# A hybrid attention and conv layer on one core: value sums emptied by VectorE, one more key block per pair through the DMA transpose, and the output projection begun inside the attention's last steps

## The chip, the core and the metric

One core of a Trainium2 chip runs the whole program. The metric is the device time of one execution in microseconds (us); for the kernel before it is the median of three runs. One further execution was recorded by the profiler, and all durations below come from it. TensorE is PE in the rows (PEld its weight loads), VectorE is DVE, ScalarE is ACT, GpSimd is POOL, and SP is the queue that issues nearly all transfers.

## What is computed

The layer has 2048 tokens of 1024 channels. Eight attention heads of 64 channels and 512 channels of a short gated convolution are computed from one projection of the normed input, joined, multiplied by `w_out` and added to the input through a gate; a feed-forward part follows.

```python
mod = (c_act @ w_ada + b_ada)[:, None, :]
sh1, sc1, g1, sh2, sc2, g2 = jnp.split(mod, N_MOD, axis=-1)
...
attn = forgetting_attention(q, k, v, logf).reshape(b, s, ATTN_WIDTH)
conv = bg * causal_dwconv(cg * xin, conv_mix_w)
mixed = jnp.concatenate([attn, conv], axis=-1)
x = x + g1 * (mixed @ w_out)
h2 = rmsnorm(x, norm2_g) * (1 + sc2) + sh2
u = causal_dwconv(h2 @ w_up, ffn_conv_w)
u_gate, u_val = jnp.split(u, 2, axis=-1)
y = (jax.nn.silu(u_gate) * u_val) @ w_down
return x + g2 * y
```

The attention is causal; a query block of 128 rows sees the key blocks up to its own, and a running sum of log-sigmoids is added to the logits before the softmax.

## The kernel before

Nearly every product is made in three passes: an operand is split into a high and a low part, and the products high by high, high by low and low by high are summed (`mm3`, L138). A split is one ScalarE copy into `hi` and one VectorE subtraction into `lo` (`split`, L865). An order that is wrapped in `K(...)` stays as the code writes it on its engine; other instructions are placed by a scheduler.

**Attention (L645 to L830).** The work is cut into 64 units, eight for each head. A unit is two query blocks, number 15-u and number u, which together see 17 key blocks. A unit goes through four stages in four successive steps of the loop at L798, so in step s four units are in work:

- `scores` of unit s (L690): PE makes the logits in chunks of up to 512 keys into four PSUM buffers (`product`, two chunks at a time), and VectorE adds the forget term and takes the maximum into `s_t` (L706), five chunks to a unit.
- `weights` of unit s-1 (L716): ScalarE forms the bias `nb` (L720) and takes the exponential of `s_t` in place, once for each of the two query blocks (L723).
- `turn` of unit s-2 (L727): the 17 blocks are transposed. The first WB = 10 go through PE (`blocks`, L743) in groups of 4, 4 and 2 into one of two PSUM buffers `pt`; ScalarE copies them to fp16 (L745), and VectorE subtracts to get the low part (`rest`, L750), which frees `pt`. The other 7 are split by GpSimd into `wide` (L734, L735) and turned by one DMA transpose from `wide` into `far` (L736, issued by SP). A reciprocal of the sums follows (L762).
- `values` of unit s-4 (L764): three products for each key block are summed into `po` (two PSUM buffers, one for each query block in turn); ScalarE empties each by one scaled copy into `at` (L781).

Inside a step the loop L823 goes round the stages, in the order turn, scores, weights, values, and lets each go on to its next `yield`; a step has five to seven rounds. Every second head, `store` (L784) turns a finished 512 columns of a pair of heads through `pt` and `tm` and writes it to `m_at` in DRAM, one piece to a step at four steps. At u = 1 to 7 of a head SP loads the next head's keys and queries, and GpSimd copies two of them (L594).

After step 63 come eight steps (s = 64 to 71) that only drain the stages.

**Output projection (`mixed`, L881).** Quarter Q takes 512 tokens. For each half `hf` of the 1024 outputs and each of eight input pieces k, in the order 4, 5, 6, 7 (from the convolution, `m_cv`) and 0, 1, 2, 3 (from the attention, `m_at`), it splits the weight piece `wo` and the input piece `src` and makes 12 products of 128x512 into four sums `acc`; pieces 2 and 3 are done together. In quarter 0 each `wo` is loaded (L908) and multiplied by the gate on GpSimd (L909) first. `mixed(0)` is called when the attention's program is at its end (L1176), followed by quarters 1 to 3 with the second norm between, and then the feed-forward part (`up`, `down`).

Of the kernel before, what the change touches and what calls it, by code (L numbers as in the profile page):

```python
# [19 lines left out]
P = 128  # L20
# [14 lines left out]
WB = 10  # L35
# [9 lines left out]
def kernel(  # L45
# [60 lines left out]
    qk = const.tile([P, 6], F32, name="qk")  # L106
# [537 lines left out]

    with ExitStack() as ph:  # L645
# [118 lines left out]
        def values(un):  # L764

            near, far = un["t"]
            h = un["h"]
            for p, (i, n, b0) in enumerate(un["parts"]):
# [11 lines left out]
                o = un["at"][:, i, (h % 2) * DH : (h % 2 + 1) * DH]  # L780
                K(A.activation(o, po, AF.Copy, scale=un["l"][:, p : p + 1]))  # L781
                yield

        def store(at, pr, chs):  # L784

            for ch in chs:
# [3 lines left out]
                tm = cp.tile([P, 512], F32, tag="tm", name="tm", bufs=2)  # L790
# [7 lines left out]
        for s in range(H * nu + 8):  # L798
# [29 lines left out]
        for g in slow:  # L828
# [10 lines left out]
    with ExitStack() as ph:  # L839
        fp = ph.enter_context(tc.tile_pool(name="fp", bufs=1))  # L840
        fp.tile([P, 32], F32, name="rim")
        fb = ph.enter_context(tc.tile_pool(name="fb", bufs=1))
# [3 lines left out]
        def raw_tile():  # L846
            return fq.tile([P, 1024], F32, tag="raw", name="raw", bufs=4)

        def pair_tiles():
            return (  # L850
                fq.tile([P, 1024], F32R, tag="hi", name="hi", bufs=4),
                fq.tile([P, 1024], F32R, tag="lo", name="lo", bufs=4),
            )

        def halves(tiles):

            return [[t[:, n * 512 : (n + 1) * 512] for t in tiles] for n in range(2)]
# [6 lines left out]

        def split(raw, hi, lo):  # L865
            A.activation(hi, raw, AF.Copy, scale=HS)  # L866
            V.tensor_tensor(lo, raw, hi.bitcast(F32), op=ALU.subtract)  # L867
            return hi, lo
# [9 lines left out]

        wo, kept = {}, {}

        def mixed(Q, side=iter(()), at=()):  # L881

            cols = slice(Q * 512, (Q + 1) * 512)
            order = (4, 5, 6, 7, 0, 1, 2, 3)
            rows = [slice((Q * 4 + t) * P, (Q * 4 + t + 1) * P) for t in range(4)]
            n = 0
            src = {}
            if Q < 2:
                spare = [(f"t{1 + i // 4}", i % 4, e) for e in "hl" for i in range(12)]
                for i, k in enumerate(order):  # L890
                    name, j, e = spare[8 * Q + i]
                    src[k] = (fb if name == "t3" else fp).tile([P, 512], F32, tag=f"{name}{j}{e}", name="src")
            else:
                for i in range(4):
                    raw = raw_tile()
                    for j in range(2):
                        src[order[2 * i + j]] = raw[:, j * 512 : (j + 1) * 512]
            if Q == 0:
                kept[0] = [raw_tile() for _ in range(4)]
                kept[1] = [wide_temp()[:, 0:D] for _ in range(4)]  # L900
            for hf in range(2):
                n0 = hf * 512
                acc = [ps_d.tile([P, 512], F32, tag="d", name="acc") for _ in range(4)]
                ops = []
                for k in order:
# [310 lines left out]
```

## Time and profile before

| what | value |
|---|---|
| median of three runs | 2559.99 us (2558.88 to 2562.83) |
| the profiled execution, its own time | 2562.44 us |
| its span, first to last instruction | 2560.5 us |
| granted TensorE clock, mean | 0.992 |
| attention, first to last `nb` (L720) | 630.8 to 963.1 us |
| first product of `mixed(0)` | 983.09 us |

The span lies within the execution's own time; 1.9 us lie around it. A row of the table of stages gives, for each engine, busy time and in brackets the number of instructions, then the granted clock, the share of the 16 DMA engines and GB/s. A row of a group gives line, engine, operation, what is written and read, the shape, the count, then busy time and the mean ns of one, and after the second bar the engine's idle time just before such instructions, with what ended it. A row of the timeline gives start, duration, engine, line, and in square brackets idle time and what ended it.

### The profile page before, as it was taken

What the parts mean: (1) busy time and instruction counts of PE and PEld (TensorE: products, weight loads), DVE (VectorE), ACT (ScalarE), POOL (GpSimd) and SP (SyncE); (2) the same over time, 40 slices, a digit from 0 to 9 for tenths busy, and PEclk for the clock granted to TensorE, in tenths of its full rate; (3) what the DMA queues carried; (4) which work ended last, traced back from release to release, by engine and by line L of the source; (5) the groups of instructions that cost most, each with busy time, mean ns of one, the idle gap of its engine ahead of it and who ended that gap; (6) DMA issues with size and microseconds to landing.
All of it is one profiled execution on the core that took longest, in us unless ns stands there. A gap on an engine that the chain in (4) does not pass through costs nothing.

```text
span 2560.5 us, 38478 instructions
## 1 busy us (share of the span) xinstructions
PE 2458.1 (96%) x14493; PEld 1995.7 (78%) x14493; DVE 1820.9 (71%) x3294; ACT 1183.2 (46%) x1932; POOL 357.8 (14%) x314
## 2 busy tenths in 40 slices
PE   4999999999999998998999999999999999999999
PEld 4988788887677776877888888877778888888887
DVE  7567874433888886676888888667768888885554
ACT  3522231111899994654444444455434444444333
POOL 4211010112656554110000000000000000000000
PEclk9999999999999999999999999999999999999999
DMA  8332563314697757332222222676632222226775
GB/s 237 140 104 59 153 177 103 99 54 122 122 187 154 162 96 236 116 111 94 83 83 74 83 83 83 210 233 209 218 125 75 86 80 81 81 84 191 226 234 188
DMA packets 400291, 341.43 MB, mean 133 GB/s; under 512 B 166545, under 2 KB 310249, under 8 KB 399081
## 3 DMA queue, kind: packets, MB, share of 16 engines
q1 hardware_dynamic: 392920, 322.13, 44.2%
q10 hardware_dynamic: 4752, 8.46, 0.9%
q0 software_dynamic: 2432, 8.39, 0.9%
q8 instruction: 113, 1.85, 0.3%
q14 instruction: 74, 0.60, 0.1%
HBM read 244.47 MB, written 65.08 MB: 121 GB/s over the span
## 4 chain that ended last, share of the span: by engine, by line
PE 50%; DVE 2%; DMA 1%; ACT 1%; issue 0%; SPq 0%; DVEq 0%; ACTq 0%
PE acc L1068 34%; PE acc L140 16%; DMA t<-x_sc 1%; DVE lo L867 1%; PE pt L956 0%; DVE t L949 0%; DVE t L876 0%; DVE t L875 0%; ACT junk L979 0%; ACT hi L866 0%; DVE b22l L867 0%; DVE lo L1023 0%; DVE t L966 0%; ACT t L958 0%; DVE w L986 0%
## 5 line engine op out<-in xcount | busy, mean ns | idle before, releaser
L140 PE MATMUL acc<-hi 128*128 128x512 f32 x960 | 378.2, 394 | 13.5 <-ACT hi L866 11.7
L140 PE MATMUL acc<-hi,lo 128*128 128x512 f32 x960 | 376.6, 392 | 0.8 <-DVE lo L867 0.7
L140 PE MATMUL acc<-lo,hi 128*128 128x512 f32 x960 | 375.9, 392 | 0.3 <-DVE lo L867 0.3
L867 DVE TENSOR_TENSOR lo<-raw,hi 128x1024 fp32r<-128x1024 f32 (+1 forms) x208 | 236.2, 1142 | 182.3 <-ACT hi L866 181.8
L866 ACT ACTIVATE hi<-raw 128x1024 fp32r<-128x1024 f32 (+1 forms) x208 | 205.0, 991 | 247.6 <-PE acc L140 207.6
L1081 DVE SCALAR_TENSOR_TENSOR w<-w,fcw,w 128x1024 f32<-128x1024 f32 x176 | 225.9, 1284 | 42.4 <-ACT w L1076 39.1
L1020 ACT ACTIVATE hi<-raw 128x1024 fp32r<-128x1024 f32 x132 | 139.4, 1057 | 221.4 <-PE acc L1068 212.7
L140 PEld LDWEIGHTS acc<-hi 128*128 128x128 f32 x960 | 181.3, 189 | 53.0 <-ACT hi L866 12.5
L140 PEld LDWEIGHTS acc<-hi,lo 128*128 128x128 f32 x960 | 181.2, 189 | 40.8 <-DVE lo L867 2.7
L140 PEld LDWEIGHTS acc<-lo,hi 128*128 128x128 f32 x960 | 181.2, 189 | 37.7 <-DVE lo L867 1.2
L1023 DVE TENSOR_TENSOR lo<-raw,hi 128x1024 fp32r<-128x1024 f32 x132 | 161.0, 1221 | 10.7 <-ACT hi L1020 10.6
L723 ACT ACTIVATE s_t<-s_t,nb,qk 128x2048 f32<-128x2048 f32 (+15 forms) x128 | 164.7, 1288 | 5.8
L140 PE MATMUL pr<-hh,wh 128*128 128x512 f32 x384 | 153.6, 400 | 0.0
L140 PE MATMUL pr<-hl,wh 128*128 128x512 f32 x384 | 151.5, 394 | 0.0
L140 PE MATMUL pr<-hh,wl 128*128 128x512 f32 x384 | 151.2, 394 | 0.0
L750 DVE TENSOR_TENSOR near<-pt,near 128x512 f16<-128x512 f32 (+1 forms) x192 | 114.9, 599 | 47.0 <-ACT near L745 47.0
L743 PE MATMUL pt<-ident,s_t 128*128 128x128 f32 x640 | 102.1, 284 | 26.2 <-DVE near L750 24.2
L706 DVE CUSTOM_DVE_ANT_0 s_t<-ps,nf,mx 128x512 f32<-128x512 f32 (+1 forms) x192 | 123.3, 642 | 2.7
L735 POOL TENSOR_TENSOR wide<-s_t,wide 128x896 f16<-128x896 f32 x64 | 121.2, 1894 | 5.4
L682 PE MATMUL ps<-kh,qs 128*128 128x512 f16 (+1 forms) x320 | 109.9, 347 | 2.0 <-ACT bt L635 1.1
L683 PE MATMUL ps<-kl,qs 128*128 128x512 f16 (+1 forms) x320 | 109.6, 347 | 0.0
L140 PE MATMUL acc<-wh,hh 128*128 128x512 f32 x256 | 103.6, 405 | 0.0
(303 smaller groups left out, 6226.0 us busy)
## 6 DMA issues: line engine op xcount, KB each, us to landing
raw<-in_w_up_dram SPq DMA_DIRECT2D x88, 512.0 KB, 3.7
raw<-y_sc SPq DMA_DIRECT2D x176, 256.0 KB, 3.9
raw<-in_w_down_dram SPq DMA_DIRECT2D x176, 256.0 KB, 4.2
y_sc<-w SPq DMA_DIRECT2D x44, 512.0 KB, 2.6
wm<-in_w_ada_dram SPq DMA_DIRECT2D x128, 128.0 KB, 2.6
wr<-in_w_in_dram SPq DMA_DIRECT2D x40, 256.0 KB, 4.3
x_t<-in_x_dram SPq DMA_DIRECT2D x16, 512.0 KB, 5.4
wa<-in_w_ada_dram SPq DMA_DIRECT2D x16, 512.0 KB, 6.4
```

What stands on the lines that cost most here:

```text
L140: ins = T.matmul(acc, lhsT=a, rhs=b, start=st, stop=sp)
L682: K(T.matmul(ps[:, 0:cw], lhsT=qt, rhs=kh[:, c0 : c0 + cw], start=True, stop=False))
L706: K(V.tensor_tensor_reduce(out=s_t[:, o0 + c0 : o0 + c0 + cw], in0=ps[:, 0:cw], in1=nf[:, c0 : c0 + cw], scale=1.0, scalar=-3.0e38 if g == ...
L723: K(A.activation(cols, cols, AF.Exp, bias=nb[:, p : p + 1], scale=qk[:, 4:5], accum_out=un["l"][:, p : p + 1]))
L735: K(G.tensor_tensor(wide[:, 1, :], s_t[:, WB * P : WU], wide[:, 0, :], op=ALU.subtract))
L750: K(V.tensor_tensor(tl, pt, th, op=ALU.subtract))
L866: A.activation(hi, raw, AF.Copy, scale=HS)
L867: V.tensor_tensor(lo, raw, hi.bitcast(F32), op=ALU.subtract)
L1020: K(A.activation(hi, raw, AF.Copy, scale=HS))
L1023: K(V.tensor_tensor(lo, raw, hi.bitcast(F32), op=ALU.subtract))
L1068: K(T.matmul(acc, lhsT=a, rhs=b, start=st, stop=sp, skip_group_check=True))
L1081: K(V.scalar_tensor_tensor(y, u[:, m : m + 1024], fcw[:, m * 44 + ct : m * 44 + ct + 1], y, op0=ALU.mult, op1=ALU.add))
```

## The change

1. `WB` goes from 10 to 9. The third group of PE transposes in `turn` has one block, not two; `wide` and `far` hold 8 blocks, not 7.
2. In `values` the two sums of a unit are emptied by VectorE with a `tensor_scalar` by the reciprocal. The order is put off: a finished sum waits in a list, and `over` empties it one round later, when the next group of four blocks has been issued, or at the stage's end.
3. `load_out` loads one piece of `w_out` in every second step of the last four heads, and GpSimd multiplies it by the gate in the step after. In the last head SP also loads the inputs 4, 5, 6, 7, 0, 1, 2 of quarter 0.
4. `mixed` is a generator that yields after every piece k. Steps 64 to 71 each take one of its pieces after the attention's own rounds, so the eight pieces of the first half stand between the draining units. Input piece 3 of quarter 0 is loaded in step 71.
5. To make room, `tm` has one buffer instead of two, `qk` lies inside `cst`, and the pool `fb` is opened ahead of the attention. The helpers of the splits move with it, unchanged.

```diff
-WB = 10
+WB = 9
...
-    qk = const.tile([P, 6], F32, name="qk")
+    qk = cst[:, 96:102]
...
+    order = (4, 5, 6, 7, 0, 1, 2, 3)
+    wo, kept, src = {}, {}, {}
+
+    def load_out(n):
+
+        hf, k = n // 8, order[n % 8]
+        n0 = hf * 512
+        wo[k, hf] = t = fb.tile([P, 512], F32, tag=f"{('b22', 't4')[k // 4]}{k % 4}{'hl'[hf]}", name="wo")
+        K(nc.sync.dma_start(t, w_out[k * P : (k + 1) * P, n0 : n0 + 512]))
+        return lambda: K(G.tensor_tensor(t, t, gates[:, n0 : n0 + 512], op=ALU.mult))
+
+    def load_mixed(Q, k):
+        cols = slice(Q * 512, (Q + 1) * 512)
+        K(nc.sync.dma_start(src[Q, k], m_at[k][:, cols] if k < 4 else m_cv[k - 4][:, cols]))
...
+    def mixed(Q, side=iter(()), at=()):
...
+            for k in order:
+                if hf == 0 and (Q or k == 3):
+                    load_mixed(Q, k)
+                (mh, ml), (wh, wl) = halves(pair_tiles())
+                split(wo[k, hf], wh, wl)
+                split(src[Q, k], mh, ml)
+                ops.append((mh, ml, wh, wl))
+                for t in () if k == 2 else range(4):
+                    for o in ops:
+                        a, b = [m[:, t * P : (t + 1) * P] for m in o[:2]]
+                        mm3(acc[t], a, b, *o[2:], k == 4, o is ops[-1] and k == 3)
...
+                if Q < 2 and n == (2, 4)[Q]:
+                    for xp, r in zip(kept[Q], rows):
+                        K(nc.sync.dma_start(xp, x[r, :]))
...
+                yield
...
+            sums = []
+
+            def over():
+                p, i, po = sums.pop(0)
+                o = un["at"][:, i, (h % 2) * DH : (h % 2 + 1) * DH]
+                K(V.tensor_scalar(o, po, un["l"][:, p : p + 1], None, op0=ALU.mult))
+
             for p, (i, n, b0) in enumerate(un["parts"]):
                 po = ps_o.tile([P, DH], F32, tag="o", name="po")
...
                     if b % 4 == 3:
                         yield
-                o = un["at"][:, i, (h % 2) * DH : (h % 2 + 1) * DH]
-                K(A.activation(o, po, AF.Copy, scale=un["l"][:, p : p + 1]))
-                yield
+                        if sums:
+                            over()
+                sums.append((p, i, po))
+            yield
+            while sums:
+                over()
...
-                tm = cp.tile([P, 512], F32, tag="tm", name="tm", bufs=2)
+                tm = cp.tile([P, 512], F32, tag="tm", name="tm", bufs=1)
...
+            if s >= (H - 4) * nu and s % 2 == 0 and s < H * nu:
+                gated = load_out((s - (H - 4) * nu) // 2)
+            if s == (H - 1) * nu:
+                places(0)
+            if (H - 1) * nu <= s < H * nu - 1:
+                load_mixed(0, order[s - (H - 1) * nu])
...
+            if (H - 4) * nu <= s < H * nu and s % 2:
+                gated()
+            if s == H * nu:
+                first = mixed(0)
+            if s >= H * nu:
+                next(first)
...
-                    if Q == 0:
-                        wo[k, hf] = fb.tile([P, 512], F32, tag=f"{('b22', 't4')[k // 4]}{k % 4}{'hl'[hf]}", name="wo")
-                        K(nc.sync.dma_start(wo[k, hf], w_out[k * P : (k + 1) * P, n0 : n0 + 512]))
-                        G.tensor_tensor(wo[k, hf], wo[k, hf], gates[:, n0 : n0 + 512], op=ALU.mult)
...
-        mixed(0)
-        mixed(1, norm2(0), (1, *range(5, 13)))
+        for _ in first:
+            pass
+        for _ in mixed(1, norm2(0), (1, *range(5, 13))):
+            pass
```

Three places show what moves. The first is VectorE in the steady attention, from the reciprocal of one step to the first subtraction of the next. `s_t` is the score tile, `mx` its maximum, `near` the low half of a PE-transposed group, `po` a value sum and `at` its place. Before:

```order
L762 RECIPROCAL l_6166<-l_6166 128x2
L706 ISA s_t_6330,mx_6331<-ps_6392,nf_5818,mx_6331 128x384
L706 ISA mx_6331 128x1
L706 ISA s_t_6438,mx_6439<-ps_6396,nf_5818 128x512
L706 ISA mx_6439 128x1
L750 TENSOR_TENSOR near_6421<-pt_6426,near_6421 128x512
```

After, with the changed kernel's own line numbers (L802 is the score chunk, L846 the subtraction, L858 the reciprocal, L869 the new emptying):

```order
L858 RECIPROCAL l_6439<-l_6439 128x2
L802 ISA s_t_6660,mx_6661<-ps_6709,nf_6028,mx_6661 128x512
L802 ISA mx_6661 128x1
L869 TENSOR_SCALAR at_6029<-po_6674,l_6219 128x64
L869 TENSOR_SCALAR at_6029<-po_6729,l_6219 128x64
L802 ISA s_t_6774,mx_6775<-ps_6743,nf_6028 128x512
L802 ISA mx_6775 128x1
L846 TENSOR_TENSOR near_6757<-pt_6762,near_6757 128x512
```

Both sums of the unit are emptied behind the last score chunk of the step and ahead of the first of the next. It is so for the five units u = 0 to 4 of a head; for u = 5 to 7 the first sum is emptied before the last chunk.

The second place is ScalarE in step 64, around the last unit's exponentials (`hi` is the high half of a split, `tm` the stored piece). Before:

```order
L720 ACTIVATE nb<-mx,qk 128x2
L723 ACTIVATE s_t,l<-s_t,nb,qk 128x1152
L723 ACTIVATE s_t,l<-s_t,nb,qk 128x1024
L745 ACTIVATE near<-pt 128x256
L791 ACTIVATE tm<-pt,vi 128x512
L781 ACTIVATE at<-po,l 128x64 x2
L745 ACTIVATE near<-pt 128x512 x2
```

After (L816 is the bias, L819 the exponential, L841 the copy to fp16, L897 the stored piece, L662 the split's copy):

```order
L816 ACTIVATE nb<-mx,cst 128x2
L662 ACTIVATE hi<-wo 128x512
L819 ACTIVATE s_t,l<-s_t,nb,cst 128x1152
L819 ACTIVATE s_t,l<-s_t,nb,cst 128x1024
L841 ACTIVATE near<-pt 128x128
L897 ACTIVATE tm<-pt,vi 128x512
L662 ACTIVATE hi<-src 128x512
```

The emptying copies are gone, and the first split of `mixed(0)` stands around the exponentials: its weight half ahead of them, its input half behind the stored piece.

The third place is SP at the attention's end. Before:

```order
L736 DMA_TRANSPOSE far<-wide 128x14x128
L792 DMA m_at_74<-tm 128x512
L908 DMA wo<-in_w_out_dram 128x512
L792 DMA m_at_74<-tm 128x512 x2
L911 DMA src<-m_cv_75 128x512
```

After (L832 is the DMA transpose, L898 the store, L724 the load of `x`, L679 the load of an input piece):

```order
L832 DMA_TRANSPOSE far<-wide 128x16x128
L898 DMA m_at_74<-tm 128x512
L724 DMA raw<-in_x_dram 128x1024 x4
L898 DMA m_at_74<-tm 128x512 x2
L679 DMA src<-m_at_74 128x512
L679 DMA src<-m_cv_75 128x512
```

The load of input piece 3 (`src<-m_at_74`) now stands behind the last two stores, those of steps 68 and 69, with one `tm` buffer between them.

More of the change, by code (lines that the diff above doesn't have):

```diff
@@ L642, with raw_tile, pair_tiles, halves @@
                 nc.scalar.dma_start(m_cv[j][:, ch * 512 : (ch + 1) * 512], y)
+    fb = end.enter_context(tc.tile_pool(name="fb", bufs=1))
+    fb.tile([P, 32], F32, name="rim")
+    def raw_tile():
+        return fq.tile([P, 1024], F32, tag="raw", name="raw", bufs=4)
+    def pair_tiles():
+        return (
+            fq.tile([P, 1024], F32R, tag="hi", name="hi", bufs=4),
+            fq.tile([P, 1024], F32R, tag="lo", name="lo", bufs=4),
+        )
+    def halves(tiles):
+        return [[t[:, n * 512 : (n + 1) * 512] for t in tiles] for n in range(2)]
@@ new lines, in load_mixed, with places @@
+    def load_mixed(Q, k):
+        cols = slice(Q * 512, (Q + 1) * 512)
+        K(nc.sync.dma_start(src[Q, k], m_at[k][:, cols] if k < 4 else m_cv[k - 4][:, cols]))
+    def places(Q):
+        for i, k in enumerate(order):
+            if Q == 0:
+                src[Q, k] = fb.tile([P, 512], F32, tag=f"t3{i % 4}{'hl'[i // 4]}", name="src")
+            elif Q == 1:
+                src[Q, k] = fp.tile([P, 512], F32, tag=f"t1{i % 4}{'hl'[i // 4]}", name="src")
+            elif i % 2 == 0:
+                raw = raw_tile()
+                for j in range(2):
+                    src[Q, order[i + j]] = raw[:, j * 512 : (j + 1) * 512]
@@ new lines, in mixed @@
+    def mixed(Q, side=iter(()), at=()):
+        rows = [slice((Q * 4 + t) * P, (Q * 4 + t + 1) * P) for t in range(4)]
+        n = 0
+        if Q:
+            places(Q)
+        if Q == 0:
+            kept[0] = [raw_tile() for _ in range(4)]
+        elif Q == 1:
+            kept[1] = [wide_temp()[:, 0:D] for _ in range(4)]
+        for hf in range(2):
+            n0 = hf * 512
+            acc = [ps_d.tile([P, 512], F32, tag="d", name="acc") for _ in range(4)]
+            ops = []
+            for k in order:
[9 more added lines that the diff above has]
+                        mm3(acc[t], a, b, *o[2:], k == 4, o is ops[-1] and k == 3)
+                if k != 2:
+                    ops = []
+                n += 1
+                if n in at:
+                    next(side, None)
+                if Q < 2 and n == (2, 4)[Q]:
+                    for xp, r in zip(kept[Q], rows):
+                        K(nc.sync.dma_start(xp, x[r, :]))
+                if Q >= 2 and k == 0:
+                    kept[Q] = [temp() for _ in range(4)]
+                    for xp, r in zip(kept[Q], rows):
+                        K(nc.sync.dma_start(xp, x[r, n0 : n0 + 512]))
+                yield
+            for t in range(4):
+                xp = kept[Q][t]
+                if Q < 2:
+                    xp = xp[:, n0 : n0 + 512]
+                V.tensor_tensor(xp, acc[t], xp, op=ALU.add)
+                if Q >= 2:
+                    G.dma_start(x1_sc[Q * 4 + t][:, n0 : n0 + 512], xp)
+                elif hf:
+                    G.dma_start(x1_sc[Q * 4 + t], kept[Q][t])
@@ L863, in wide_temp @@
             return fp.tile([P, 1040], F32, tag="w4", name="w4", bufs=5)[:, 0:1026]
[L865 to L868, printed above, removed]
         def add_gated(acc, gate, src, dst):
```

77 lines of the change are left out of this document (8 added, 69 removed).

## Prediction

> **What bounds the kernel now.** I began with the page of the profile and its chain.
>
> ```profile
> span 2560.5 us, 38478 instructions
> PE 2458.1 (96%) x14493; PEld 1995.7 (78%) x14493; DVE 1820.9 (71%) x3294; ACT 1183.2 (46%) x1932; POOL 357.8 (14%) x314
> 1181.03 0.09 issue
> ```
>
> PE is busy nearly throughout, but matmuls overlap in the record, so 96% does not say that nothing can be won. The last line is the first piece of the chain that ended last: it reaches back only to 1181 us, and the change lies before that. So the stages must be read by themselves. The table of stages for the attention, its drain, and the first two halves of `mixed(0)`:
>
> ```profile
> core 0: us, PE busy (x) PEld busy (x) DVE busy (x) ACT busy (x) POOL busy (x), PEclk, DMA share, GB/s
> 640.00:960.00 320.00, 297.53 (x4429) 229.18 (x4428) 276.78 (x849) 289.18 (x615) 197.50 (x135) 1.00 0.73 144
> 965.30:975.30 10.00, 7.85 (x175) 7.09 (x175) 2.28 (x6) 6.40 (x17) 2.83 (x2) 1.00 0.84 172
> 975.30:983.09 7.79, 0.00 (x0) 0.00 (x0) 0.71 (x2) 2.09 (x4) 1.26 (x1) 0.67 0.51 166
> 983.09:1008.50 25.41, 24.83 (x96) 19.70 (x97) 22.36 (x21) 10.88 (x19) 19.41 (x13) 0.90 1.03 387
> 1008.50:1030.40 21.90, 21.90 (x98) 17.95 (x96) 14.97 (x22) 11.33 (x21) 5.72 (x6) 1.00 0.26 99
> ```
>
> In the attention three engines are busy 86 to 93% and none is full: they wait for each other in a ring. Behind it PE stands still for 7.79 us, and its next 96 products take 25.41 us, 3.5 more than the following 98. The waits of 640 to 960 us, and the count of units:
>
> ```profile
> DVE near L750 <- ACT near L745: 41.0, 62, 1.1
> PEld pt L743 <- DVE near L750: 31.5, 60, 1.1
> ACT at L781 <- PE po L777: 10.9, 27, 0.6
> L720 ACT ACTIVATE nb<-mx,qk x64: 287/297/298, 630.8 to 963.1; 128x2 f32<-128x2 f32 x64
> ```
>
> The last row gives the mean unit: (963.1 - 630.8) / 63 = 5.27 us. The first two name the ring: VectorE waits for ScalarE's fp16 copy of the third transposed group, PE waits for VectorE to free the buffer, and ScalarE's next copy waits for PE. Two turns of it in the timeline, ScalarE first, then VectorE, then PE:
>
> ```profile
> 700.42 0.36 ACT L745 ACTIVATE near<-pt 128x256 f16<-128x256 f32 x1
> 701.27 0.31 ACT L781 ACTIVATE at<-po,l 128x64 f32<-128x64 f32 x1 [0.29 <-PE po L777]
> 701.74 1.08 ACT L745 ACTIVATE near<-pt 128x512 f16<-128x512 f32 x2 [0.16 <-PE pt L743]
> ...
> 705.68 0.36 ACT L745 ACTIVATE near<-pt 128x256 f16<-128x256 f32 x1
> 706.33 0.59 ACT L745 ACTIVATE near<-pt 128x512 f16<-128x512 f32 x1
> 707.25 0.60 ACT L745 ACTIVATE near<-pt 128x512 f16<-128x512 f32 x1 [0.32 <-PE pt L743]
> ...
> 710.70 0.36 ACT L745 ACTIVATE near<-pt 128x256 f16<-128x256 f32 x1
> ```
>
> ```profile
> 706.07 0.43 DVE L750 TENSOR_TENSOR near<-pt,near 128x256 f16<-128x256 f32 x1 [0.74 <-ACT near L745]
> 706.41 0.74 DVE L706 CUSTOM_DVE_ANT_0 s_t<-ps,nf,mx 128x512 f32<-128x512 f32 x1
> ```
>
> ```profile
> 706.55 0.66 PE L743 MATMUL pt<-ident,s_t 128*128 128x128 f32 x4 [0.68 <-DVE near L750]
> ```
>
> From the copy at 705.68 to the same copy at 710.70 is 5.02 us, the ring with nothing else in it: 0.36 copy, 0.43 subtraction, 0.66 transposes, then from 707.25 on 3.45 us of ScalarE (copy, bias, two exponentials). The turn before, 700.42 to 705.68, took 5.26; there PE came late with its transposes, and the two emptyings and their waits filled that time.
>
> **The change, part by part.** Prices, from the groups by shape, and one row of the gate's group with min, median and max:
>
> ```profile
> L750 DVE TENSOR_TENSOR near<-pt,near 128x512 f16<-128x512 f32 x122 | 83.7, 686 | 0.8 <-ACT near L745 0.8
> L750 DVE TENSOR_TENSOR near<-pt,near 128x256 f16<-128x256 f32 x60 | 25.5, 425 | 40.2 <-ACT near L745 40.1
> L706 DVE CUSTOM_DVE_ANT_0 s_t<-ps,nf,mx 128x256 f32<-128x256 f32 x24 | 11.4, 475 | 0.5
> L706 DVE DVE_READ_ACCUMULATOR2_ANT mx<- 128x1 f32 x303 | 25.2, 83 | 0.0
> L762 DVE RECIPROCAL l<-l 128x2 f32<-128x2 f32 x60 | 9.6, 160 | 0.0
> L781 ACT ACTIVATE at<-po,l 128x64 f32<-128x64 f32 x118 | 33.2, 304 | 11.0 <-PE po L777 10.9
> L735 POOL TENSOR_TENSOR wide<-s_t,wide 128x896 f16<-128x896 f32 x64 | 121.2, 1894 | 5.4
> L734 POOL TENSOR_SCALAR wide<-s_t 128x896 f16<-128x896 f32 x64 | 60.0, 938 | 132.2 <-ACT s_t L723 129.6 <-DVE mx L706 2.1
> L594 POOL TENSOR_SCALAR kh<-kh 64x2048 f16<-64x2048 f16 x8 | 15.1, 1892 | 7.6 <-DMA kh<-k_hi 7.0
> L909 POOL TENSOR_TENSOR wo<-wo,gates x16: 1260/1720/1835, 976.0 to 1011.0; 128x512 f32<-128x512 f32 x16
> ```
>
> *One block fewer on PE.* VectorE's subtraction costs 686 ns at 512 columns and 425 at 256, 1.02 ns a column: 294 ns at 128, so 0.13 less in the ring. ScalarE's copy goes from 0.36 to about 0.24 by the same line through its 0.59 and 0.36, 0.12 less. The ring shrinks from 5.02 to 4.77. PE is spared one of the transposes: four take 0.66 with the last one's tail, so 0.16 at most, and I use 0.10.
>
> *The emptyings leave ScalarE.* That frees 2 x 0.304 a unit, but in the turn above ScalarE was waiting for PE at 707.25 anyway, so most of it lies beside work. It pays where ScalarE waited for PE's sums with copies behind it: 10.9 us in 27 places, 0.18 a unit at most.
>
> *VectorE takes them.* By the same line 64 columns cost 0.23. Its busy time a unit is 276.78 / 320 x 5.27 = 4.56; with 0.46 more and 0.13 less, 4.89. Neighbours overlap, though: the chunk at 706.41 starts 0.09 before the subtraction ends, and two more instructions so overlapped give 4.71. Both stand close to the ring's 4.77. The Trainium skill ("VectorE: DVE Perf Modes", the section on the TRN2 errata) prices a PSUM-to-SBUF operation at 120 cycles plus one per column at 0.96 GHz; for 64 columns that is an estimate of 0.19 us, with which the load would be 4.81 without overlap. No row here shows the shape, and the sum goes by the line.
>
> *GpSimd and the DMA transpose.* Eight blocks for seven: (0.938 + 1.894) x 8/7 = 3.24 a unit. In the last four heads a gate of 1.26 to 1.84 falls on every second unit, and two key copies of 1.89 on seven heads' eight units (0.47). Together at most 4.63, below the unit. The gate waits for a load issued a step earlier, and behind it on GpSimd's queue stands the next `wide`, behind that SP's transpose and the far blocks; these are needed two steps later, about 10 us, against 3.24 and some 5 of transfer. I put this at nothing; without that cover, the two units of a head with both key copies and a gate of 1.72 would take GpSimd 3.78 + 6.48 + 1.72 = 11.98 against two units of 4.99, so 2 us once in a head.
>
> So a unit loses 0.25 in the ring. Where the unit was longer than the ring, 5.27 against 5.02 on average, PE's 0.10 and ScalarE's 0.18 bound what changes. I take 0.28: **64 x 0.28 = 18 us**. The bounds are 0.10 (only the transpose counts, 6) and 5.27 - 4.71 = 0.56 (VectorE full, 36).
>
> *The drain.* The rows that time the first product of `mixed(0)`, first on ScalarE, then PE; then the stored piece's copy and two lines of transfer time (the `m_at` stores, then the loads of input pieces, min/median/max):
>
> ```profile
> 963.52 1.35 ACT L723 ACTIVATE s_t<-s_t,nb,qk 128x1152 f32<-128x1152 f32 x1
> ...
> 966.09 0.36 ACT L745 ACTIVATE near<-pt 128x256 f16<-128x256 f32 x1
> ...
> 982.41 0.63 ACT L866 ACTIVATE hi<-src 128x512 fp32r<-128x512 f32 x1 [4.45 <-DMA src<-m_cv]
> ```
>
> ```profile
> 966.96 0.77 PE L743 MATMUL pt<-ident,s_t 128*128 128x128 f32 x5 [1.71 <-DVE near L750]
> ```
>
> ```profile
> L791 ACT ACTIVATE tm<-pt,vi x16: 665/680/689, 711.0 to 975.4; 128x512 f32<-128x512 f32 x16
> DMA to landing us min/median/max: 2.5/4.6/6.6
> DMA to landing us min/median/max: 3.9/4.4/6.9
> ```
>
> Before, the first product waited for a load until 983.09. Now loads and gates are done early, and the first product waits for ScalarE: at 963.52 comes the weight's copy (0.63), the exponentials (966.09 - 963.52 = 2.57), the copy 0.24, the stored piece 0.68, the input's copy 0.63: 968.3, while PE is through with step 64 at 965.2 (the last row: 966.96 less 1.71), a gap of 3 us. From there 96 products (21.9 us at the later rate) and the attention's remaining PE work (7.85) stand in one row. A second gap follows. Input piece 3 is loaded behind two stores that share one `tm`: 0.68, landing (2.5 to 4.6, I take 3.5), 0.68, two issues (0.4, an estimate), load 4.2, copy 0.63, together 10.1 us after the first store's transposes; PE has two pieces, four transposes and three products for that time, 2.7 + 0.65 + 2.7 + 0.7 = 6.75. So 3.35 us are lost, 2.0 to 7.1 by the rows' ends. 968.3 + 21.9 + 7.85 + 3.35 = 1001.4 against 1008.5: **7 us**, between 3 and 12 (neither gap).
>
> The granted clock was 0.67 in the idle stretch and 0.90 over the 96 products behind it. The Trainium skill ("TensorE: Matmul & The Clock Gate", Part 1) says that an idle window of about 3.4 us halves the clock until a window as long was busy; the trace agrees so far. By it my gaps, 3.0 and 3.35, stand at the edge, and each that trips would cost about 1.7 us more: an estimate of 3.6 instead of 7 for the drain.
>
> Sum: 2562.4 - 18 - 7 = 2537 for the profiled execution. The median of the runs lies 2.4 below that execution, so I say **2535**.
>
> **Rivals.**
>
> 1. *The ring opens altogether.* With ScalarE ahead, VectorE is never kept waiting and runs at 4.71. For it: all 41.0 us of VectorE's wait come from ScalarE's third copy. Against: the ring is still 4.77, and PE's heavy steps stay. 36 + 11 = 47: 2513.
> 2. *Only the drain counts.* The units stay at 5.27, less PE's transpose that falls into waits, because VectorE fills up to 4.89 and the store and key steps come on top. Then 2560 - 7 = 2553. For it: VectorE's upper price; against: the 0.25 out of the ring's own rows.
> 3. *PE waits for the sums, slower.* For five of eight units the first sum is emptied only behind the step's last score chunk, and PE's first value product of the next unit needs that PSUM buffer; all score products and transposes stand behind it. From the subtraction that frees `pt`, VectorE needs two chunks with their reads, the reciprocal and one emptying, 0.74 + 0.48 + 2 x 0.08 + 0.16 + 0.23 = 1.8 us; PE arrives after four transposes, some 0.5, or later where score products come first. So it waits up to 1.3 us, in the mean of all units at most 0.8. PE idles 31.5 / 61 = 0.52 a unit today at the transposes, which can hide it, so I expect most of it covered. It decides from an uncovered mean of 0.39 (0.28 and the drain's 7 / 64): above that the kernel is slower. Half-way to the end, at 0.58, it costs 12 us: 2572.
>
> **How the numbers follow.** Forecast 0.60, rival 1 0.17, rival 2 0.11, rival 3 0.12. The forecast's own bounds run from 2560 - 30 - 12 = 2518 to 2560 - 6 - 3 = 2551; with rivals 1 and 2 taken in, 2513 to 2556. Rival 3 stays out, with the ends of the rest. About 0.2% (5 us) is what a measurement can tell from no change. Faster than that: the forecast, rival 1 and part of rival 2, 0.80; within it 0.07, from rivals 2 and 3; slower 0.13.
>
> **What would show it.** In the new profile the mean unit should be about 4.99 us with the shortest near 4.77; `at` on VectorE at 0.2 us; VectorE's wait for ScalarE's third copy far below 41 us; PE's first `mixed` product near 950 (968.3 - 18), and its 97th near 983. Two gaps of about 3 us should stand before the first product and before piece 3. I am wrong if the unit stays above 5.2, if PE waits for `at` by more than 0.4 a unit, or if PE waits for `far`.

## The result and the profile after

| | before | changed |
|---|---|---|
| median, four runs each | 2559.43 us | 2540.24 us (2537.63 to 2544.29) |
| ratio, with its 95% interval | | 0.9924 (0.9907 to 0.9942) |
| span of the profiled execution | 2560.5 us | 2540.1 us |

The kernel became 0.76% faster, 19 us, where 25 were forecast. But the time did not come from where the prediction put it. The page of the changed kernel begins so:

```profile
span 2540.1 us, 38347 instructions
PE 2429.5 (96%) x14429; PEld 1988.7 (78%) x14429; DVE 1827.2 (72%) x3422; ACT 1147.2 (45%) x1804; POOL 375.7 (15%) x314
```

The attention lies between the first and the last `nb`; this is its row in the changed kernel:

```profile
L816 ACT ACTIVATE nb<-mx,cst x64: 287/297/299, 628.6 to 973.9; 128x2 f32<-128x2 f32 x64
```

It takes 345.3 us, against 332.3 before: 13 us longer, where 18 less were forecast. Split at this row and at counted products (the 97th of `mixed(0)`, the first of `up`, the first of `down`, the last of `up`), the two executions stand so:

| stretch | before | changed | difference |
|---|---|---|---|
| up to the first `nb` | 630.8 | 628.6 | -2.3 |
| attention, first to last `nb` | 332.3 | 345.3 | +13.0 |
| on to the 97th output product | 45.4 | 41.1 | -4.3 |
| on to the first `up` product | 171.0 | 169.4 | -1.6 |
| first `up` part, to the first `down` product | 445.4 | 432.8 | -12.6 |
| on to the last `up` product | 691.2 | 678.0 | -13.2 |
| the rest | 244.3 | 245.0 | +0.7 |

The first line is within what this part varies by (627.8 to 631.6 in the runs below). The two `up` parts, whose code the change does not touch, gain 25.8 us, more than the whole change; all the rest together loses 5.5. Two stretches of 100 us in them, first of the kernel before, then of the changed one, in the columns of the stage table:

```profile
1300.00:1400.00 100.00, 100.00 (x431) 80.38 (x430) 83.18 (x93) 45.69 (x72) 0.00 (x0) 1.00 0.25 79
2000.00:2100.00 100.00, 100.00 (x430) 80.42 (x429) 82.62 (x92) 45.16 (x62) 0.00 (x0) 1.00 0.25 79
```

```profile
1300.00:1400.00 100.00, 100.00 (x443) 82.82 (x442) 85.87 (x96) 46.27 (x73) 0.00 (x0) 1.00 0.25 81
2000.00:2100.00 100.00, 100.00 (x443) 82.82 (x442) 85.50 (x96) 45.03 (x63) 0.00 (x0) 1.00 0.26 84
```

PE is called 100% busy in all four at a granted clock of 1.00, and yet it makes 443 products in 100 us where it made 431. From start to start (the median over the part's products) that is 227 ns against 234, and 3696 x 7 ns is the 26 us that the table shows. PE's busy share doesn't show this; the count beside it does.

Now the attention. The waits of the changed kernel from 640 to 960 us:

```profile
ACT near L841 <- PE pt L839: 55.1, 58, 3.2
DVE near L846 <- ACT near L841: 37.2, 49, 1.9
ACT tm L897 <- DMA m_at<-tm: 11.3, 5, 3.1
PE pt L839 <- ACT tm L897: 9.8, 5, 2.8
PE po L878 <- DVE at L869: 1.5, 5, 0.3
```

The third row is new: ScalarE waits for the store before it can fill the one `tm` buffer again. In the starts of the `nb`, heads 2, 4 and 6, which carry the store steps, take 47.3, 48.6 and 47.3 us (42.9, 42.7 and 42.7 before), while the odd heads take 42.10 (42.37). The first row shows ScalarE waiting 55 us for PE's transposes; in the kernel before, over the same 320 us, it was a quarter of that:

```profile
ACT near L745 <- PE pt L743: 13.3, 57, 0.7
```

Two units of an odd head, ScalarE:

```profile
783.51 0.29 ACT L816 ACTIVATE nb<-mx,cst 128x2 f32<-128x2 f32 x1
...
786.46 0.25 ACT L841 ACTIVATE near<-pt 128x128 f16<-128x128 f32 x1
788.02 1.08 ACT L841 ACTIVATE near<-pt 128x512 f16<-128x512 f32 x2 [1.31 <-PE pt L839]
788.99 0.30 ACT L816 ACTIVATE nb<-mx,cst 128x2 f32<-128x2 f32 x1
...
793.29 0.60 ACT L841 ACTIVATE near<-pt 128x512 f16<-128x512 f32 x1 [0.59 <-PE pt L839]
793.78 0.29 ACT L816 ACTIVATE nb<-mx,cst 128x2 f32<-128x2 f32 x1
```

The short unit takes 793.78 - 788.99 = 4.79 us, the forecast ring. The long one before it takes 5.48, where it took 5.25: these two units make 10.27 us, as before. (In an odd head of the changed kernel three units of eight are short, 4.78 each, as three were before, 5.02; the other five take 5.03 to 6.10.) In that long unit VectorE has no pause from 783.18 to 791.51; its only one is in the short unit:

```profile
792.25 0.29 DVE L846 TENSOR_TENSOR near<-pt,near 128x128 f16<-128x128 f32 x1 [0.74 <-ACT near L841]
```

In the kernel before, the long unit of the two turns (700.42 to 705.68) had one, of 0.50 us:

```profile
700.81 0.42 DVE L750 TENSOR_TENSOR near<-pt,near 128x256 f16<-128x256 f32 x1 [0.50 <-ACT near L745]
```

The prices of the changed instructions in this trace, by shape:

```profile
L846 DVE TENSOR_TENSOR near<-pt,near 128x128 f16<-128x128 f32 x58 | 16.9, 291 | 31.0 <-ACT near L841 30.0
L841 ACT ACTIVATE near<-pt 128x128 f16<-128x128 f32 x58 | 14.7, 253 | 0.0
L869 DVE TENSOR_SCALAR at<-po,l 128x64 f32<-128x64 f32 x114 | 28.8, 278 | 0.2 <-PE po L880 0.2
```

A duration overlaps the next instruction. Two emptyings and what follows them:

```profile
787.96 0.47 DVE L869 TENSOR_SCALAR at<-po,l 128x64 f32<-128x64 f32 x2
788.34 0.68 DVE L802 CUSTOM_DVE_ANT_0 s_t<-ps,nf 128x512 f32<-128x512 f32 x1
```

From the start of an emptying to the next start is 0.196 us (the median of 114), so a unit's two take some 0.39 us of VectorE.

The drain, PE's first output products:

```profile
978.52 0.80 PE L140 MATMUL acc<-hi 128*128 128x512 f32 x1 [2.18 <-ACT hi L662]
979.11 0.63 PE L140 MATMUL acc<-lo,hi 128*128 128x512 f32 x1
981.17 0.79 PE L140 MATMUL acc<-hi,lo 128*128 128x512 f32 x1 [1.43 <-DVE lo L663]
...
1009.76 0.50 PE L140 MATMUL acc<-hi 128*128 128x512 f32 x1 [2.02 <-ACT hi L662]
```

The two forecast gaps are there: 2.18 us ahead of the first product, with 1.43 more ahead of the third, and 2.02 ahead of piece 3. The stage rows around the first gap, in which PE's last value product ends at 976.34:

```profile
976.30:978.40 2.10, 0.04 (x2) 0.00 (x0) 0.74 (x4) 2.10 (x6) 1.04 (x1) 1.00 0.91 171
978.40:981.20 2.80, 1.25 (x3) 0.53 (x3) 2.70 (x2) 2.80 (x7) 2.14 (x1) 0.50 0.57 153
```

The granted clock was halved at 978.4, after 2.1 us without a product and before the second gap, and it was still 0.50 in the stage row from 981.2 to 985.0 us; behind the gap of 2.02 us it stayed at 1.00. The Trainium skill ("TensorE: Matmul & The Clock Gate", Part 1) has the clock halve behind an idle window of some 3.4 us; this trace shows the halving after a shorter one.

### The profile page after: what moved, and what is told of

Its sections match the earlier page's. It is cut to its first block, busy times and chain, and to the rows that moved or that the text cites. A ratio compares the mean times of both kernels' runs of the same rounds, so it can differ in the third digit from the quotient of the medians.

```text
span 2540.1 us, 38347 instructions
## 1 busy us (share of the span) xinstructions
PE 2429.5 (96%) x14429; PEld 1988.7 (78%) x14429; DVE 1827.2 (72%) x3422; ACT 1147.2 (45%) x1804; POOL 375.7 (15%) x314
## 4 chain that ended last, share of the span: by engine, by line
PE 49%; DVE 2%; DMA 1%; ACT 1%; issue 0%; SPq 0%; DVEq 0%; ACTq 0%
PE acc L1103 33%; PE acc L140 15%; DMA t<-x_sc 1%; DVE lo L663 1%; PE pt L991 0%; DVE t L984 0%; DVE t L974 0%; ACT hi L662 0%; DVE t L973 0%; ACT junk L1014 0%; DVE lo L1058 0%; DVE raw L1052 0%; DMA out_dram<-t 0%; DVE b22l L663 0%; SPq L1199 0%
## 5 line engine op out<-in xcount | busy, mean ns | idle before, releaser
L662 ACT ACTIVATE hi<-raw 128x1024 fp32r<-128x1024 f32 (+1 forms) x208 | 205.1, 991 | 248.4 <-PE acc L140 206.1
L819 ACT ACTIVATE s_t<-s_t,nb,cst 128x2048 f32<-128x2048 f32 (+15 forms) x128 | 164.7, 1287 | 5.7
L846 DVE TENSOR_TENSOR near<-pt,near 128x512 f16<-128x512 f32 (+1 forms) x192 | 106.1, 554 | 44.5 <-ACT near L841 43.2
L831 POOL TENSOR_TENSOR wide<-s_t,wide 128x1024 f16<-128x1024 f32 x64 | 136.6, 2134 | 5.3
L839 PE MATMUL pt<-ident,s_t 128*128 128x128 f32 x576 | 96.9, 288 | 35.0 <-DVE near L846 23.4
L802 DVE CUSTOM_DVE_ANT_0 s_t<-ps,nf,mx 128x512 f32<-128x512 f32 (+1 forms) x192 | 122.7, 639 | 1.2
L841 ACT ACTIVATE near<-pt 128x512 f16<-128x512 f32 (+1 forms) x192 | 87.2, 480 | 59.0 <-PE pt L839 57.9
```

What stands on the lines that cost most here:

```text
L802: K(V.tensor_tensor_reduce(out=s_t[:, o0 + c0 : o0 + c0 + cw], in0=ps[:, 0:cw], in1=nf[:, c0 : c0 + cw], scale=1.0, scalar=-3.0e38 if g == ...
L819: K(A.activation(cols, cols, AF.Exp, bias=nb[:, p : p + 1], scale=qk[:, 4:5], accum_out=un["l"][:, p : p + 1]))
L831: K(G.tensor_tensor(wide[:, 1, :], s_t[:, WB * P : WU], wide[:, 0, :], op=ALU.subtract))
```

## The experiments

Kernels are compared by their ratio to runs of the kernel before on the same chip.

### Where the gain of the unchanged part comes from

The built programs give each tile's address. Before, the moving operands of the `up` products lie 32 bytes past a multiple of 512 (b11 at 89120), nearly all of them; after, at multiples (130048). Their stationary operands `hi` and `lo` lie at multiples in both (196096). The 32 bytes are the tile `qk`, which the change moved into `cst`. So, the kernel before with this alone:

```diff
-    qk = const.tile([P, 6], F32, name="qk")
+    qk = cst[:, 96:102]
```

> The kernel before with one line of the change: the six-column tile qk becomes a slice of cst, so every tile allocated after it on that side lies 32 bytes lower and the moving operands of the up products lie at multiples of 512 bytes, as their stationary operands do. Theory A (placement: the change's gain sits in the spacing of the 3696 up products, 234 ns before and 227 ns after, and comes from the addresses): spacing 227 ns except at t1l (still 320 bytes off, 176 products), so about 3500 x 7 ns = 24.5 us less there, 2 us less ahead of the attention as in the changed kernel, attention and output products unchanged: 2560 - 26.5 = 2533 us, faster than the changed kernel. Theory B (the up products run faster because of what the change did to the attention or the output products, or because of the state of the core): spacing stays 234 ns, time 2558 to 2560 us.

Measured: 2538.88 us, ratio 0.9915 (0.9898 to 0.9931). One line gives the whole gain of the change. It is 6 us short of the expectation: products of t1 and t3 had medians of 228 to 232 ns, all others 227. t1's low half was still 320 bytes off; why t3, which is at multiples, slows too is not explained. In this run, the first of the two stretches of 100 us:

```profile
1300.00:1400.00 100.00, 100.00 (x441) 82.44 (x440) 83.66 (x94) 45.21 (x71) 0.00 (x0) 1.00 0.25 79
```

The reverse, the changed kernel with `qk` as a tile of its own:

```diff
-    qk = cst[:, 96:102]
+    qk = const.tile([P, 6], F32, name="qk")
```

> The changed kernel with qk a tile of its own again, and nothing else: all left-hand tiles lie 32 bytes higher. Theory A (placement): the up products go back to 234 ns, 3696 x 7 ns = 26 us more, and 2 us more ahead of the attention: 2540 + 28 = 2568 us, so without this line the change is slower than the kernel before by some 8 us. Theory B (the attention and output product edits make the gain): spacing 227 ns, 2540 us.

Measured: 2565.70 us, ratio 1.0022 (1.0013 to 1.0032), and 431 products again:

```profile
1300.00:1400.00 100.00, 100.00 (x431) 80.31 (x430) 83.02 (x92) 45.48 (x75) 0.00 (x0) 1.00 0.26 84
```

Without this line all the rest of the change makes the kernel slower. The third run of this group puts offsets from 32 to 384 bytes under twelve pairs of operands and leaves the others alone:

```diff
+            if name in ("b11", "b21", "t2") and (name, k) not in bt:
+                fp.tile([P, 8], F32, name=f"pad{name}{k}")
```

> The changed kernel with a pad of 32 bytes ahead of each of twelve pairs of moving operands of the up products (b11, b21 and t2, four each), so that these lie 32, 64, 96 and so on to 384 bytes past a multiple of 512, while t1, t3, t4 and b22 stay at multiples. Theory A (what counts is where a product's moving operand lies against its stationary operand): the products of t1, t3, t4, b22 keep 227 ns, those of b11, b21, t2 vary with the offset, 234 ns at 32 bytes, between 226 and 235 ns elsewhere. Theory B (the spacing is set by the elementwise work beside it, whose tiles do not move here): all groups stay at 227 ns.

Measured: 2559.89 us in the one run. Start to start, by the offset of the moving operand past a multiple of 512 (about 130 products each, 2101 at zero, spacings above 400 ns left out; ns):

| offset | 0 | 32 | 64 | 96 | 128 | 160 | 192 | 224 | 256 | 288 | 320 | 352 | 384 |
|---|---|---|---|---|---|---|---|---|---|---|---|---|---|
| median | 227 | 236 | 226 | 233 | 233 | 234 | 235 | 232 | 228 | 236 | 229 | 234 | 233 |

In one and the same program the unmoved operands keep 227 and the moved ones go from 226 to 236. No other tile moved in this run. So the address counts, not the elementwise work beside it. No simple rule comes out (the low half at 128 bytes took 241, the high half at 320 took 225, and t3 above was slow at a multiple), and the offset of the stationary operand was not varied. The two `up` parts are 10.5 us longer than in the changed kernel's profile; the other 7.6 us of this run lie elsewhere and are not explained.

### The long heads

Two `tm` buffers, with room from smaller `mx`, `nb` and `l`:

```diff
-                tm = cp.tile([P, 512], F32, tag="tm", name="tm", bufs=1)
+                tm = cp.tile([P, 512], F32, tag="tm", name="tm", bufs=2)
```

> The changed kernel with two tm buffers again, room for which comes from smaller mx, nb and l pools. Theory A (with one tm buffer ScalarE waits for the store of the previous chunk, and that store is issued on SP behind transposing DMAs that wait for GpSimd): heads 2, 4 and 6 fall from 47.3, 48.6, 47.3 us to the 42.1 us of the odd heads plus the work of the store steps, some 42.4 us, so about 16 us less: 2524 us. Theory B (those heads are long because the steps of the store themselves, or GpSimd's gate multiplies, are late, whatever the number of buffers): heads 2, 4, 6 stay above 46 us, time 2538 to 2541 us.

Measured: 2525.23 us, ratio 0.9865 (0.9851 to 0.9880). Heads 2, 4 and 6 take 42.23 us, and the attention 328.9:

```profile
L816 ACT ACTIVATE nb<-mx,cst x64: 287/297/298, 628.2 to 957.1; 128x2 f32<-128x2 f32 x64
```

So the single buffer cost 16.4 us of attention. The waits for the store sum to 11.3 us only. The granted clock is the likely rest. In the changed kernel it was 0.97 over the attention's stage row, where it was 1.00 before and is 1.00 with two buffers; it fell to 0.50 inside the gaps of 2.46, 2.76 and 2.40 us that the three longest waits left on PE, and stayed there behind them. The stage row and the three stretches:

```profile
640.00:960.00 320.00, 286.84 (x4206) 217.96 (x4206) 277.99 (x927) 245.71 (x475) 228.48 (x145) 0.97 0.87 170
739.50:742.80 3.30, 3.05 (x16) 1.88 (x17) 1.73 (x4) 2.49 (x5) 1.89 (x1) 0.50 0.94 214
828.30:835.00 6.70, 5.89 (x48) 4.21 (x49) 3.67 (x11) 4.78 (x9) 3.57 (x3) 0.50 1.06 210
896.50:903.20 6.70, 6.00 (x50) 4.31 (x51) 3.55 (x9) 4.74 (x9) 1.58 (x3) 0.50 1.05 307
```

How much of the 16.4 us the halved clock took was not measured by itself. Why the buffer comes free late is to be seen on SP in the changed kernel, at the first pair of stores:

```profile
706.02 2.97 SPq L832 DMA_TRANSPOSE far<-wide  x1
709.04 1.07 SPq L585 DMA_DIRECT2D qs<-q_lo  x1
710.16 0.59 SPq L585 DMA_DIRECT2D kl<-k_lo  x1
710.79 0.59 SPq L898 DMA_DIRECT2D m_at<-tm  x1
```

ScalarE had filled `tm` by 708.6; the store was issued 2.2 us later, behind a transposing DMA that holds the queue for 3 us and two loads. The fill that waited longest stood behind a store that was issued 4.0 us late. With one buffer still, but the store on another queue:

```diff
-                nc.sync.dma_start(m_at[pr][:, ch * 512 : (ch + 1) * 512], tm)
+                nc.scalar.dma_start(m_at[pr][:, ch * 512 : (ch + 1) * 512], tm)
```

> The changed kernel with its one tm buffer, whose store is issued from ScalarE's queue instead of SP's. Theory A (on SP the store stands behind transposing DMAs that wait for GpSimd, and so the buffer comes free late): heads 2, 4 and 6 fall from 47.3, 48.6 and 47.3 us to 42.3 to 44 us, ScalarE waits for the store at most 3 us a time, time 2525 to 2532 us. Theory B (the store's own time is what one buffer can't hide): heads 2, 4 and 6 stay above 46 us, time 2537 to 2541 us.

Measured: 2523.43 us in the one run, heads 2, 4 and 6 at 42.2 us; ScalarE's wait for the store is gone from the waits. One buffer is enough; the store's place on SP's queue is what cost 16 us. The Trainium skill ("DMA: Bandwidth & Descriptors", section "Issuing engines are not separate DMA queues") says that issuing from several engines saves only the sequencer's time of starting a DMA, usually little. Here that time, of the DMAs ahead of the store, was the whole cost: up to 4.0 us, where a store itself took 2.3 to 3.0 us from issue to landing.

### What sets two units

With two `tm` buffers the pair still takes 10.27 us. I first held PE's continuous work in the long unit for the cause, and left a third of the value products out (the share of the weights' low half is then missing from the output):

```diff
-                    K(T.matmul(po, lhsT=t[:, 0, :], rhs=vl, start=False, stop=False))
-                    K(T.matmul(po, lhsT=t[:, 1, :], rhs=vh, start=False, stop=b == n - 1))
+                    K(T.matmul(po, lhsT=t[:, 0, :], rhs=vl, start=False, stop=b == n - 1))
```

> The version with two tm buffers (2525.2 us, units of 5.49 and 4.78 us in turn in the middle of the odd heads), with the third value product of every key block left out: the output then lacks the share of the low half of the weights. TensorE has 17 products of some 0.036 us less per unit, 0.61 us, ScalarE, VectorE and GpSimd have the same work. Theory A (in the long unit TensorE has no pause between its last wait and the transposes that ScalarE waits for, so TensorE sets it): the long unit falls by 0.3 to 0.6 us, to 4.9 to 5.2 us, the short one stays near 4.78 us, ScalarE's wait for the transposes falls from 49 us by 10 to 17 us, time 2508 to 2516 us. Theory B (the long unit is set on ScalarE or VectorE, or by the ring around the third copy as well): 5.49 and 4.78 us stay within 0.1 us, time 2522 to 2526 us.

Measured: 2521.43 us in the one run; the long unit 5.32, the short 4.78. Of 0.61 us only 0.17 came through, about half of the least expected. The waits from 640 to 940 us, first with two `tm` buffers, then with fewer products:

```profile
ACT near L841 <- PE pt L839: 48.9, 57, 1.5
DVE near L846 <- ACT near L841: 25.7, 45, 1.0
PE pt L839 <- DVE near L846: 20.7, 45, 0.7
```

```profile
ACT near L841 <- PE pt L839: 44.7, 60, 1.4
PE pt L839 <- DVE near L846: 32.1, 62, 0.9
DVE near L846 <- ACT near L841: 19.6, 39, 1.0
```

PE's saved time turned into waiting for VectorE to free `pt`, 20.7 to 32.1 us. My theory fell for the most part: behind PE stands VectorE, which the last edit below tests. Next, the two edits to the units one at a time. First `WB` back, sums still on VectorE:

```diff
-WB = 9
+WB = 10
```

> The version with two tm buffers (2525.2 us) with WB back at 10, so that the third group turned by TensorE has two blocks: the value sums still go through VectorE, and the output products still begin during the last units. The third copy takes 0.36 us instead of 0.25, its subtraction 0.43 instead of 0.29. Theory A (TensorE holds the sum of two units): the short unit grows by some 0.2 to 0.25 us, the long one shrinks by about as much or holds, and two units stay within 0.1 us of 10.27, or grow by the two transposes at most, 0.22 us: attention 1 to 7 us longer, time 2526 to 2532 us. Theory B (the ring's length is what each unit pays, as predicted): 0.24 us on every unit, 64 x 0.24 = 15 us: 2540 us.

Measured: 2536.67 us, ratio 0.9915 (0.9901 to 0.9930), between the two expectations. The short unit is 5.02 us, the long 5.60, a pair 10.62: the ring's 0.24 in the short unit, and 0.11 in the long one. Its short unit equals that of the kernel before, so the sums' leaving ScalarE took nothing off it, and its odd heads take 43.50 us against 42.37. Then `WB` 9 and the sums on ScalarE again:

```diff
-                K(V.tensor_scalar(o, po, un["l"][:, p : p + 1], None, op0=ALU.mult))
...
+                K(A.activation(o, po, AF.Copy, scale=un["l"][:, p : p + 1]))
```

> The version with two tm buffers (2525.2 us) with the value sums evicted by ScalarE again, as in the kernel before, and WB still 9. Theory A (the sums were never in the ring that sets the short unit, and on VectorE they lengthen the long unit, in which VectorE has no pause): the short unit stays at 4.78 us, the long one falls from 5.49 to between 5.0 and 5.25 us, attention 7 to 13 us shorter, time 2512 to 2518 us. Theory B (ScalarE's 0.3 us evictions lengthen the ring, as predicted): short unit 4.9 to 5.0 us, and the attention 3 to 7 us longer: 2528 to 2532 us.

Measured: 2523.83 us, ratio 0.9856 (0.9839 to 0.9872). The short unit stays at 4.79, the long one falls to 5.23, as theory A has it. ScalarE's waits are again for the sums, and little for PE:

```profile
DVE near L846 <- ACT near L841: 39.1, 59, 1.3
ACT at L877 <- PE po L873: 11.5, 25, 1.5
ACT near L841 <- PE pt L839: 8.1, 47, 0.4
```

The time fell less than expected, and no more than noise below that with two `tm` buffers alone (2525.23), because two units of heads 4 and 6 took 9.34 and 8.23 us, where such a unit takes 5.90 in head 2; PE waits for `far` there, 4.0 us in all. One odd head (from its first `nb` to that of the next), in all four cases:

| | sums on ScalarE | sums on VectorE |
|---|---|---|
| WB 10 | 42.37 us (before) | 43.50 us |
| WB 9 | 41.11 us | 42.10 us (changed) |

One block fewer on PE is worth 1.3 to 1.4 us a head; the sums on VectorE cost 1.0 to 1.1.

### The drain, and what follows

Output products not between the last units, but behind them, with loads and gates still early:

```diff
-            if s >= H * nu:
-                next(first)
```

> The version with two tm buffers (2525.2 us) without the steps of the output products between the last units: they begin behind the attention, while the early loads and gates of w_out and the loads of the operands stay. Theory A (the interleaving itself takes TensorE's pauses of the last units): first output product 10 to 16 us later, the 97th 4 to 6 us later, time 2529 to 2532 us. Theory B (what counted was that w_out was loaded and gated early): first product later, but the 97th within 1.5 us, time 2524 to 2527 us.

Measured, from two `tm` buffers on: 2522.07 us, ratio 0.9853 (0.9837 to 0.9870). Against expectation this is not slower. First products of the two:

```profile
961.73 0.79 PE L140 MATMUL acc<-hi 128*128 128x512 f32 x1 [2.18 <-ACT hi L662]
```

```profile
972.84 0.48 PE L140 MATMUL acc<-hi 128*128 128x512 f32 x1
```

The first product comes 11 us later, the 97th 2.9 us earlier (994.7 against 997.6). From the last `nb` the 97th took 45.4 us before, 40.6 with the steps, 36.9 without: the steps cost 3.7, and the rest of the change is worth 8.5. Ten blocks for nine leave it at 40.0 (with the steps), and sums on ScalarE at 36.9 (without, next run), so I put the 8.5 to the early loads and gates; no run has them alone. The clock may be a part of the 3.7: with the steps it was 0.60 from 961.7 to 970.0 us, the first products; without, 0.73 from 967.0 to 972.8 us and 1.00 from the first product on. The same edit with the sums on ScalarE:

> The version before it (value sums on ScalarE, WB 9, two tm buffers), also without the steps of the output products between the last units. Theory A (the steps put 1.2 us splits in front of the last units' work on ScalarE and VectorE, and cost more than TensorE's pauses give): the 97th output product 2 to 4 us earlier, 2509 to 2515 us. Theory B (with ScalarE's sums the last units' pauses are other ones, and the steps now pay): 2 to 4 us later than the version before it.

Measured: 2519.39 us, ratio 0.9838 (0.9823 to 0.9853), beside 2523.83 with the steps on the same chip; 36.9 us again against 40.8. Part of that difference is that one of the two units that waited for `far` was short here. Then, on this version, one more block for the DMA, with one `tm` buffer and the store on ScalarE's queue:

```diff
-WB = 9
+WB = 8
```

> As the version before it, with WB 8 (nine of 17 blocks turned by DMA, no third group on TensorE), one tm buffer and the store issued from ScalarE's queue, which frees the room. Theory A (the third copy and its subtraction are what the short unit waits for): short unit from 4.78 to between 4.3 and 4.6 us, where TensorE's own 4.6 us of work takes over; attention 5 to 12 us shorter. Theory B (GpSimd, at 3.7 to 4.3 us a unit before and 0.4 us more now, or the DMA's transposes, become late and TensorE waits for far): units above 5 us, time over 2515 us.

Measured: 2516.70 us in two runs, ratio 0.9829 (0.9809 to 0.9849), no clear gain on the version before it. Theory A's short unit came, 4.32 us, but its shorter attention did not (325.6 us against 324.5), and theory B's long units came with it: six of 63 rose to between 7.8 and 10 us, with PE waiting for `far`, 22.6 us in all:

```profile
PEld L873 <- DMA far<-wide: 26.2, 17, 3.7
PE po L873 <- DMA far<-wide: 22.6, 14, 3.6
```

Last, `WB` 9, sums on ScalarE, products behind the attention, two `tm` buffers and the store on ScalarE's queue:

> Value sums on ScalarE, WB 9, two tm buffers, output products behind the attention (2519.4 us before, with one unit of 8.01 us among units of 4.8 to 5.9), and now the store of the turned sums issued from ScalarE's queue. Theory A (in the one long unit TensorE waits for far because its transposing DMA stands on SP in a row with the stores): no unit above 6 us outside the change of heads, attention 2 to 4 us shorter, 2515 to 2518 us. Theory B (far is late because GpSimd, which also gates w_out and copies the next head's keys, makes wide late): one or two units of 8 us remain, 2517 to 2521 us.

Measured: 2517.51 us, ratio 0.9828 (0.9814 to 0.9841). The attention takes 323.7 us. One unit of 7.01 us is left; PE still waited 1.1 us for `far` there, so neither theory alone covers it, and what makes `far` late (GpSimd's gates and key copies, or SP's queue) stays open. This version beats both kernels, by 1.7% the one and by some 1% the other.

## Why the prediction was right and wrong

The sum came out near the measurement by luck: two errors of opposite sign, each larger than the whole effect. The attention was 31 us off (13 lost, 18 forecast as gain), and the 25.8 us of the `up` parts were in no term.

- **What was missing.** The step "What bounds the kernel now" looked at the attention and its drain alone, and "The change, part by part" has no word on the move of `qk`, which stands in the list of the change and in its diff. That line is worth 23 us alone and 25 in the changed kernel (its two runs). No row of the trace of before showed the mechanism; the addresses in the built program would have shown that tiles move.
- **The ring: 64 x 0.28 = 18 us.** The rows were right: 4.79 us for 4.77, 253 and 291 ns for 240 and 294. The step that failed is "So a unit loses 0.25 in the ring": in an odd head only three units of eight are set by it. The long unit shown had VectorE at work with a pause of 0.50 us, and the change took the pause. Alone, with two `tm` buffers, both edits gave 3.4 us of attention.
- **The emptyings** were put at up to 0.18 us a unit of gain. They were no gain in the short unit, and on VectorE they cost about 1 us a head. The price was not what failed: the duration is 278 ns for 230, but the spacing is 0.196 us. The Trainium skill ("VectorE: DVE Perf Modes", the section on the TRN2 errata) gives an estimate of 0.19 us; the trace agrees with it as a spacing, not as a duration. The prediction held VectorE's load against the mean unit, and the mean does not tell that, of the two units shown, its longer pause lies in the short one.
- **One `tm` buffer** was priced in the drain, with 2 us of gap where it lay (3.35 forecast), but not for the twelve stores before it, where it cost 16.4 us. The eighth block of the transposing DMA was priced on GpSimd and in transfer, but not in the time for which the DMA holds SP's queue: a median of 1.5 us before and 2.9 in the changed kernel.
- **The drain, 7 us:** 4.3, within its bounds. The gaps were found with the forecast causes and smaller; one of the two halved the clock, though both were put at the edge of doing so. Already before, 0.67 over 7.79 us without a product means 5.1 us at half, so the clock fell some 2.6 us after PE stopped, sooner than the 3.4 us that the prediction held the trace to agree with. The 0.4 us for two issues rests on no row; before, the issue of a store took 0.32 us or more, so two take 0.65. That the interleaving pays was wrong, by 3.7 us; that its splits stand ahead of the attention's last copies on ScalarE and VectorE is the cause that I see in the order of the code, and no run shows it by itself.
- **GpSimd and `far` at nothing:** right for the changed kernel, which shows no wait for `far` in the attention. Where the units get shorter it is next.
- **Rivals.** PE's wait for `po` is 1.5 us in all, so the third fell. The first needed a VectorE that is never kept waiting; it still waits 37 us. The second (units stay at 5.27, only the drain counts) comes nearest to the attention once `tm` is mended: 5.22. As it stands, the mean unit is 5.48, past the 5.2 at which the prediction called itself wrong, and PE's first output product comes at 978.5 us, where 950 was forecast.
- **The range.** The lower end of the forecast's own bounds takes 30 us for the units where the sum above it has 36; the stated range, 2513 to 2556, has rival 1's 36 in it and does not depend on this.

## What to carry to other kernels

A change that adds, moves or drops a tile moves the addresses of all that follow; count the products in a fixed stretch of an unchanged stage before crediting the edits, and give the placement an experiment of its own. Where steps alternate between two kinds, price a moved instruction in each kind: an engine with a low mean may have no pause in the one that matters. Before halving a buffer, see what stands ahead of its release on the queue that empties it.

## What the hardware showed unexpectedly

- Products of 128x512 fp32r with a granted clock of 1.00 start every 227 ns with operands at multiples of 512 bytes (231 for t3 in one run), and every 225 to 241 ns (medians) with the moving operand elsewhere. The Trainium skill ("SBUF — State Buffer", section "Who interferes with whom") gives TensorE independent read ports for the moving operand and the weight load. That section says nothing of an address. The runs say that the address matters, and not whether the weight load is what the moving operand collides with.
- A transposing DMA holds SP's queue, and whatever is issued behind it waits that long: 1.8 to 6.9 us with eight blocks (median 2.9 of 64 in the changed kernel), 1.5 to 4.4 with seven (median 1.5, before).
- The granted clock fell to 0.50 inside four gaps of PE of 2.18 to 2.76 us in the changed kernel, 1.7 to 2.2 us behind the last product, and rose 3.4 or 6.8 us later; a gap of 2.02 us left it at 1.00.
